# The second feed-forward's end in an order of its own, with a shorter inverse root, in an encoder layer on one core

## The chip, the core and the metric

The kernel runs on one core of a Trainium2 chip. TensorE (PE in the profile) multiplies matrices, VectorE (DVE), ScalarE (ACT) and GpSimd (POOL) work on elements, and SyncE (SP) issues nearly all DMAs. SBUF is the working memory of 128 partitions, PSUM holds the eight banks into which PE accumulates. The metric is the device time of one execution in microseconds (us): the median of three runs before the change, and beside it one profiled execution, whose trace all rows come from.

## The reference

One encoder layer is applied to two sequences of 512 tokens by 1024 channels, with the same weights: `y_prompt` from `x_prompt`, `y_sample` from `x_sample`.

```
x = x + 0.5 * swiglu(rms_norm(x, ffn1_norm), ...)            # first feed-forward
h = rms_norm(x, mix_norm); proj = h @ w_in; ...              # attention and mLSTM memory, merged
x = x + merged @ w_out
x = x + 0.5 * swiglu(rms_norm(x, ffn2_norm), ...)            # second feed-forward
return rms_norm(x, final_norm)

rms_norm(x, g) = x * rsqrt(mean(x * x, axis=-1) + 1e-6) * g
swiglu(x, wg, wu, wd) = (silu(x @ wg) * (x @ wu)) @ wd       # inner width 2816
```

Each query and key head, each memory head and the first three norms need an inverse root too.

## The kernel before, in words

**Stages.** The first feed-forward treats both sequences together; then come the mixing blocks of the two sequences (attention with eight heads, the mLSTM memory with four, gates, output projection), which overlap by hand; then the second feed-forward, and the final norm at its end. All matrix products are made of a high and a low part in `float32r`, three matmuls per product.

**The feed-forwards.** Gate/up and down products use a seven-product scheme (Strassen-Winograd) over the two sequences and the two halves of the inner dimension: B11, B21, B22, T4, T1, T2_, T3. `ffn_down` (line 449) runs the down product in the order of `DOWN`: B11, B21, T2_, T3, T4, T1, B22, for four chunks of the inner dimension, 28 steps in all. Each step fills four PSUM banks, d = 0 to 3, one for each block of 128 tokens, 128 partitions by 512 channels. `flush_` (line 542) evicts a bank as soon as it is finished, adding 0.5 times the bank to an accumulator in SBUF (line 550, a `scalar_tensor_tensor` of VectorE). T1 and B22 share the same banks, B22 accumulating on top of T1, so a bank goes on with B22 when its T1 sum has been read.

**The end of the last chunk.** In the last seven steps `flush_` calls `done(s, h, d)` when half h (512 channels) of block d of sequence s is complete: (0, 0) behind B21, (0, 1) behind T4, (1, 1) behind T1, and (1, 0) behind B22, the last step. For the second feed-forward this is `done2` (line 1346). It squares the half on ScalarE with a sum per row (`square`, line 1160), multiplies it by its half of `final_norm` in place (line 1349: on VectorE for (1, 0), else on GpSimd), and, when the blocks concerned are complete, makes the row scale (`row_scale`, line 1169, then `rstd_cols`) for four blocks of the first sequence or for two of the second, scales whole blocks of 1024 channels (line 1363 on ScalarE; line 1361 on VectorE for the last block of the second sequence) and stores each block with one DMA of SyncE (line 1364, 512 KB).

**The inverse root.** `rstd_cols` (line 151) takes sums of squares, one column for each block or head, divides by the width and adds 1e-6 (line 159), makes a first guess by integer operations on the bits (lines 161 and 163) and sharpens it three times (lines 167, 168, 170): 1 + 2 + 9 = 12 small operations of VectorE, each waiting for the one before. It is called 21 times: twice at the head (`norm_x`, where the inputs are normed before they are transposed), in the norms between the stages, for query and key heads, once for each memory head (`mem_out`, whose result PE then spreads over the partitions at line 187), and three times at the end. Its tiles come from pools of five buffers for each width.

**What sets the order.** A scheduler places the instructions on each engine's queue by a priority, which follows the order of the program text; `shifted` moves it, and `pin` (`tc.keep_in_program_order`) keeps pinned instructions in the order of the text among themselves. Each engine then works its queue strictly in order. The attention of the first sequence stands between 690 and 830 us: scores at line 914, their maxima at 917, transposes of the weights at 935 and products with the values at 942; the queries' transposes are at line 856, behind the rotation (lines 725 to 736) and the split (line 591), and matmuls of gates (line 686) are dealt in between.

Of the kernel before, what the change touches and what calls it, by code (L numbers as in the profile page):

```python
# [16 lines left out]
P = 128  # L17
S = 512
D = 1024
# [3 lines left out]
EPS = 1e-6  # L23
# [3 lines left out]
def encoder(ctx, tc, I, outs):  # L27
    nc = tc.nc
# [5 lines left out]
    spool = ctx.enter_context(tc.tile_pool(name="spool", bufs=4))  # L34
# [7 lines left out]
    def nm(s):  # L42
        n_id[0] += 1
        return f"{s}_{n_id[0]}"
# [100 lines left out]
    def emit_hl(src, g, k, xh, xl):  # L145
# [2 lines left out]
                                       op0=ALU.mult, op1=ALU.subtract)  # L148
        return i1, i2

    def rstd_cols(v, width, n):


        def t_(dt=F32):
            w = max(width, 4)
            return spool.tile([P, w], dt, tag=f"rs{w}", bufs=5, name=nm("rs"))[:, 0:width]
        V = nc.vector
        a = t_()
        V.tensor_scalar(a, v, 1.0 / n, EPS, op0=ALU.mult, op1=ALU.add)
        b = t_(I32)  # L160
        V.tensor_scalar(b, a.bitcast(I32), 1, None, op0=ALU.logical_shift_right)
        y_ = t_(I32)
        V.tensor_scalar(y_, b, -1.0, 1597463007.0, op0=ALU.mult, op1=ALU.add)
        y = y_.bitcast(F32)
        for _ in range(3):
            t = t_()
            V.scalar_tensor_tensor(t, y, -0.5, y, op0=ALU.mult, op1=ALU.mult)
            V.tensor_tensor(t, t, a, op=ALU.mult)
            r = t_()
            V.scalar_tensor_tensor(r, t, 1.5, y, op0=ALU.add, op1=ALU.mult)  # L170
            y = r
        return y

    def col_sums(acc, bs=(0, 1, 2, 3)):
        p = PT()
# [42 lines left out]
    V_ = nc.vector  # L218
    G_ = nc.gpsimd
    HK_ = KD // 2  # L220

    B11, B21, B22, T4, T1, T2_, T3 = range(7)
# [223 lines left out]
    DH = KD // 2  # L446
    n_steps = len(DOWN) * len(CHUNKS)

    def ffn_down(wd, rb, ring, tail, xres, done, at_step, hook):
# [88 lines left out]
        def add(t, u):  # L538
            V_.tensor_tensor(t, t, u, op=ALU.add)

        def flush_(i, d, p):
            m, last = DOWN[i % 7], i >= n - 7
            acc = {B11: e16[:, d], T2_: e16[:, DH + d], T1: e5[:, d], B21: xs[0][:, d], T4: xs[0][:, DH + d],
                   T3: xs[1][:, DH + d], B22: xs[1][:, d]}[m]
            if last and m == T1:
                acc = xs[1][:, DH + d]
            if i < 7 and m in (B11, T2_, T1):
                nc.scalar.activation(acc, p, AF.Copy, scale=0.5)
            else:
                V_.scalar_tensor_tensor(acc, p, 0.5, acc, op0=ALU.mult, op1=ALU.add)  # L550
# [583 lines left out]
    pin = tc.keep_in_program_order  # L1134
# [3 lines left out]
    x2buf = [dpool.tile([P, 2, 4, S], F32, name=f"x2buf{s}") for s in range(2)]  # L1138
    rbuf = [[dpool.tile([P, 7, 2, S], F32, name=f"rbuf{n}_{j}") for j in range(NF // 2)] for n in range(2)]
# [3 lines left out]
    up = Up(xc, I["ffn1_w_gate"], I["ffn1_w_up"], rbuf[0])  # L1143
# [14 lines left out]
    def square(x, to):  # L1158

        nc.scalar.activation(T2(F32, "f2"), x, AF.Square, accum_out=to)  # L1160

    def sums_tile():
        return spool.tile([P, 2, 4], F32, tag="sqs", bufs=6, name=nm("sqs"))

    def row_scale(sq, n=slice(0, 4)):

        w = n.stop - n.start
        t = spool.tile([P, 4], F32, tag="cs4", bufs=4, name=nm("rsum"))[:, 0:w]
        V_.tensor_tensor(t, sq[:, 0, n], sq[:, 1, n], op=ALU.add)
        return rstd_cols(t, w, D)  # L1170
# [97 lines left out]
    def done1(s, h, b):  # L1268
        x_ = xs[s][:, h * 4 + b, :]
        nc.sync.dma_start(xbuf[s][:, h, b, :], x_)  # L1270
# [51 lines left out]
    up = Up(xc, I["ffn2_w_gate"], I["ffn2_w_up"], rbuf[1])  # L1322
# [15 lines left out]
    tail = up.rest(raw0)  # L1338
    fn = []
# [3 lines left out]
        for half in range(2):  # L1343
            nc.gpsimd.dma_start(fn[half], I["final_norm"][half * S:(half + 1) * S].partition_broadcast(P))

    def done2(s, h, b):
        x_ = xs[s][:, h * 4 + b, :]
        square(x_, ssq3[s][:, h, b:b + 1])
        (V_ if (s, h) == (1, 0) else G_).tensor_tensor(x_, x_, fn[h], op=ALU.mult)
        if s == 0 and h == 1 and b == 3:  # L1350
            n = slice(0, 4)
        elif s == 1 and h == 0 and b % 2:
            n = slice(b - 1, b + 1)
        else:
            return
        r = row_scale(ssq3[s], n)
        for i in range(n.start, n.stop):
            v = xs[s].rearrange("p (h b) c -> p h b c", h=2)[:, :, i, :]
            r_ = r[:, i - n.start:i - n.start + 1]
            if s and i == 3:  # L1360
                V_.tensor_scalar(v, v, r_, None, op0=ALU.mult)
            else:
                nc.scalar.activation(v, v, AF.Copy, scale=r_)
            nc.sync.dma_start(outs[s][0, i * P:(i + 1) * P, :].rearrange("p (h c) -> p h c", h=2), v)

    ffn_down(I["ffn2_w_down"][0], rbuf[1], up.ring, tail, lambda s, h: x2buf[s][:, h], done2, n_steps - 14, load_fn)


def host_consts():
# [62 lines left out]
```

## Time and profile before

| what | us |
|---|---|
| median of three runs | 2118.5 (2116.89 to 2118.99) |
| profiled execution, its own time | 2116.6 |
| span of the profiled execution | 2114.8 |
| TensorE busy in it | 2068.3 (98%) |
| VectorE busy | 1558.7 (74%) |
| ScalarE busy | 940.2 (44%) |
| last matmul's end | 2100.4 |
| last operation's end (ScalarE's scaling) | 2109.0 |

The span runs from the first instruction to the last; the 1.8 us around it belong to the execution's own time. A row of the timeline gives start, duration, engine, line, operation, output and input, and in square brackets how long the engine was idle before and what ended that. A row of stretches gives, for a piece of the span, its length and then the busy time with the number of instructions of PE, of its weight loads, of VectorE, ScalarE and GpSimd, the clock granted to TensorE, the DMA engines' busy share and GB/s. A row of a group gives the count, the busy time, the mean duration in ns and the idle time before.

### The profile page before, as it was taken

How to read it: one execution, taken by the hardware profiler on the slowest of the kernel's cores; microseconds unless marked ns; L12 is line 12 of the kernel's file. 1: busy time of each engine (PE TensorE's matmuls, PEld its weight loads, DVE VectorE, ACT ScalarE, POOL GpSimd, SP SyncE). 2: the span in 40 equal slices, each digit the busy share in tenths (PEclk: the TensorE clock that was granted, in tenths of full speed). 3: DMA queues.
4: the chain of work that ended last, by engine and by line, in shares of the span. 5: the costliest groups of instructions: out<-in, count | busy, mean ns of one | idle time of the engine just before them, and what ended most of it. 6: DMA issues, size and time to landing. Idle time of an engine off the chain costs nothing.

```text
span 2114.8 us, 26230 instructions
## 1 busy us (share of the span) xinstructions
PE 2068.3 (98%) x9472; PEld 1692.4 (80%) x9472; DVE 1558.7 (74%) x2583; ACT 940.2 (44%) x1565; POOL 103.2 (5%) x110
## 2 busy tenths in 40 slices
PE   6999999999999999999999999999999999999997
PEld 5888888888888777878887787788888888888885
DVE  7888787776796896574649855754887877786696
ACT  6443443442225566463436555544544434343223
POOL 1000000001000110000101101010000000000002
PEclk9999999999999999999999999999999999999999
DMA  7464653489764222232341222354546545379763
GB/s 268 151 223 166 209 179 140 148 325 379 266 229 140 76 75 77 82 119 83 111 160 59 72 97 72 130 164 163 171 163 205 198 160 179 130 277 396 264 212 123
DMA packets 137425, 361.76 MB, mean 171 GB/s; under 512 B 13296, under 2 KB 13312, under 8 KB 136272
## 3 DMA queue, kind: packets, MB, share of 16 engines
q1 hardware_dynamic: 136704, 358.83, 48.6%
q0 software_dynamic: 592, 1.27, 0.2%
q8 instruction: 74, 1.21, 0.2%
q14 instruction: 55, 0.45, 0.1%
HBM read 255.15 MB, written 104.89 MB: 170 GB/s over the span
## 4 chain that ended last, share of the span: by engine, by line
PE 86%; DVE 7%; ACT 3%; DMA 2%; issue 1%; SPq 0%; POOL 0%; DVEq 0%; ACTq 0%; POOLq 0%
PE pss L283 17%; PE mm L686 14%; PE pst L283 11%; PE mm L283 10%; PE mm L533 7%; PE mm L670 4%; PE pst L533 4%; PE pss L533 4%; PE mm L1115 3%; PE pso L533 2%; PE pso L942 2%; PE pso L670 1%; PE pso L1071 1%; PE pss L914 1%; PE pss L1022 1%; PE pso L1115 1%
## 5 line engine op out<-in xcount | busy, mean ns | idle before, releaser
L283 PE MATMUL pss<-xc,w 128*128 128x512 f32 x1584 | 379.1, 389 | 0.0
L283 PEld LDWEIGHTS pss<-xc,w 128*128 128x128 f32 x1584 | 297.2, 188 | 62.0 <-DVE t L313 0.2
L686 PE MATMUL mm<-xh,w 128*128 128x512 f32 x896 | 294.1, 397 | 0.0
L283 PE MATMUL mm<-xc,w 128*128 128x512 f32 x1056 | 254.7, 391 | 2.9 <-ACT f L292 2.2
L242 ACT ACTIVATE w<-wr 128x1024 fp32r<-128x1024 f32 x132 | 139.7, 1060 | 235.3 <-PE pst L283 142.0
L283 PEld LDWEIGHTS mm<-xc,w 128*128 128x128 f32 x1056 | 196.7, 188 | 47.8 <-ACT f L292 6.3
L205 DVE TENSOR_TENSOR w<-wr,w 128x1024 fp32r<-128x1024 f32 (+1 forms) x112 | 136.6, 1221 | 114.1 <-ACT w L204 108.9
L243 DVE TENSOR_TENSOR w<-wr,w 128x1024 fp32r<-128x1024 f32 x132 | 161.1, 1222 | 80.2 <-ACT w L242 79.9
L686 PEld LDWEIGHTS mm<-xh,w 128*128 128x128 f32 x896 | 167.8, 189 | 32.4
L533 PE MATMUL mm<-w,rt 128*128 128x512 f32 x792 | 185.6, 389 | 0.9 <-DMA rt<-rbuf 0.9
L686 PE MATMUL mm<-xl,w 128*128 128x512 f32 x448 | 177.5, 396 | 0.0
L533 PEld LDWEIGHTS mm<-w,rt 128*128 128x128 f32 x792 | 148.4, 188 | 32.2 <-DMA rt<-rbuf 1.5
L204 ACT ACTIVATE w<-wr 128x1024 fp32r<-128x1024 f32 (+1 forms) x112 | 114.6, 1030 | 113.5 <-PE pso L1115 35.0
L283 PE MATMUL pst<-xc,w 128*128 128x512 f32 x528 | 127.1, 389 | 0.0
L283 PE MATMUL pst<-xc,f 128*128 128x512 f32 x528 | 127.0, 389 | 0.0
L283 PEld LDWEIGHTS pst<-xc,w 128*128 128x128 f32 x528 | 99.0, 188 | 20.8 <-ACT t L316 0.3
L283 PEld LDWEIGHTS pst<-xc,f 128*128 128x128 f32 x528 | 99.1, 188 | 20.6
L590 ACT ACTIVATE w<-t 128x512 fp32r<-128x512 f32 x82 | 51.6, 632 | 121.8 <-PE pst L533 63.6
L590 ACT ACTIVATE w<-wr 128x512 fp32r<-128x512 f32 x72 | 44.6, 631 | 129.8 <-PE pso L533 65.7
L686 PEld LDWEIGHTS mm<-xl,w 128*128 128x128 f32 x448 | 84.6, 189 | 16.2
L533 PE MATMUL pss<-w,rt 128*128 128x512 f32 x396 | 95.2, 390 | 1.3 <-ACT w L590 1.3
L533 PE MATMUL pst<-w,rt 128*128 128x512 f32 x396 | 94.3, 389 | 0.0
(323 smaller groups left out, 3497.8 us busy)
## 6 DMA issues: line engine op xcount, KB each, us to landing
rt<-rbuf SPq DMA_DIRECT2D x154, 512.0 KB, 6.2
rbuf<-t SPq DMA_DIRECT2D x72, 512.0 KB, 3.2
wr<-in_ffn_w_gate_dram SPq DMA_DIRECT2D x56, 512.0 KB, 4.2
wr<-in_w_in_cols_dram SPq DMA_DIRECT2D x56, 512.0 KB, 3.5
wr<-in_ffn_w_up_dram SPq DMA_DIRECT2D x44, 512.0 KB, 3.5
rbuf<-f SPq DMA_DIRECT2D x30, 512.0 KB, 3.2
rbuf<-tab SPq DMA_DIRECT2D x30, 512.0 KB, 3.6
wr<-in_ffn_w_down_dram SPq DMA_DIRECT2D x48, 256.0 KB, 7.6
```

What stands on the lines that cost most here:

```text
L204: pin(nc.scalar.activation(hi, raw, AF.Copy))
L205: pin(lo_eng.tensor_tensor(lo, raw, f(hi), op=ALU.subtract))
L242: pin(nc.scalar.activation(t[:, 0], src, AF.Copy))
L243: pin(V_.tensor_tensor(t[:, 1], src, f(t[:, 0]), op=ALU.subtract))
L283: nc.tensor.matmul(p, a[:, k, :], xt[:, b, k, :], start=(first and k == 0 and i == 0), stop=(k == HK_ - 1 and i == 2), skip_group_check=True)
L533: nc.tensor.matmul(p, r[:, b, d * P:(d + 1) * P], u[:, a, :], start=(first and q == 0 and k == 0), stop=(q == len(us) - 1 and k == 2), ski ...
L590: nc.scalar.activation(hi, src, AF.Copy)
L670: nc.tensor.matmul(p[b][:, :N], a[:, k, bs], w_[:, kl, :], start=(k == 0 and i == 0), stop=(k == KD - 1 and i == 2))
L686: nc.tensor.matmul(p, a[:, k, :], b, start=(k == 0 and i == 0), stop=(k == n - 1 and i == 2))
L914: nc.tensor.matmul(p, qT[:, h, b * P:(b + 1) * P], kv[:, hk * 2 + j, :], start=(j == 0), stop=(j == 1))
L942: nc.tensor.matmul(po, Vst[:, kv_, hk, :], w, start=(kv_ == 0 and i == 0), stop=(kv_ == 3 and i == 1))
L1115: nc.tensor.matmul(p[b], a[:, k, bs], w_[:, k - k0, :], start=(k == 0 and i == 0), stop=(k == KD - 1 and i == 2))
```

## The change

The inverse root is split into `rs_tile`, `rstd_of` (which takes a pinning function) and `rstd_cols`. Behind the first guess it now makes one Newton step (three operations) and one step of third order (five), 11 operations with the first.

`ffn_down` gets an `ends` function for the last step, B22, of the last chunk; the first feed-forward has none. `done2` keeps the first sequence's squares and GpSimd multiplications, but holds its row scale back; behind T1's block b it squares that half, multiplies it into a spare tile (`e5`) on VectorE, and scales and stores block b of the first sequence. `ends2` does B22's blocks: eviction, square and multiplication into another tile (`e16`); behind block 1 a root for blocks 0 and 1 from the two sums of squares (`last_scale`); behind block 2 the scaling and storing of block 0 in two halves. Block 3 is evicted in two halves of 256 columns, one squared by ScalarE and one by VectorE; then block 1's halves are scaled, the root of blocks 2 and 3 is made, and their four halves are scaled and stored: half 0 of block 3 by one operation of VectorE that also multiplies by `final_norm`, half 1 of block 2 by VectorE, the two others by ScalarE, which also issues their stores itself. Stores of the second sequence are 256 KB each. These operations are pinned.

```diff
+    def rstd_of(a, width, pin=lambda i: i):
...
+        b = t_(I32)
+        pin(V.tensor_scalar(b, a.bitcast(I32), 1, None, op0=ALU.logical_shift_right))
+        y_ = t_(I32)
+        pin(V.tensor_scalar(y_, b, -1.0, 1597463007.0, op0=ALU.mult, op1=ALU.add))
+        y = y_.bitcast(F32)
+        t = t_()
+        pin(V.scalar_tensor_tensor(t, y, -0.5, y, op0=ALU.mult, op1=ALU.mult))
+        pin(V.tensor_tensor(t, t, a, op=ALU.mult))
+        pin(V.scalar_tensor_tensor(t, t, 1.5, y, op0=ALU.add, op1=ALU.mult))
+        y, t, p, q = t, y, b.bitcast(F32), t_()
+        pin(V.tensor_tensor(t, y, y, op=ALU.mult))
+        pin(V.tensor_tensor(t, t, a, op=ALU.mult))
+        pin(V.tensor_scalar(p, t, 0.375, -1.25, op0=ALU.mult, op1=ALU.add))
+        pin(V.tensor_tensor(p, p, t, op=ALU.mult))
+        pin(V.scalar_tensor_tensor(q, p, 1.875, y, op0=ALU.add, op1=ALU.mult))
+        return q
...
     def rstd_cols(v, width, n):
...
-        for _ in range(3):
-            t = t_()
-            V.scalar_tensor_tensor(t, y, -0.5, y, op0=ALU.mult, op1=ALU.mult)
-            V.tensor_tensor(t, t, a, op=ALU.mult)
-            r = t_()
-            V.scalar_tensor_tensor(r, t, 1.5, y, op0=ALU.add, op1=ALU.mult)
-            y = r
-        return y
+        a = rs_tile(width)
+        nc.vector.tensor_scalar(a, v, 1.0 / n, EPS, op0=ALU.mult, op1=ALU.add)
+        return rstd_of(a, width)
...
+            if last and m == B22 and ends:
+                ends(d, p, acc, e16, e5)
+                return
...
             elif m == T1:
-                done(1, 1, d)
+                done(1, 1, d, e5)
...
-    def done2(s, h, b):
+    half_ms, other_r = [None], []
+
+    def store(s, i, h, v, q=None):
+        return (q or nc.sync).dma_start(outs[s][0, i * P:(i + 1) * P, h * S:(h + 1) * S], v)
+
+    def done2(s, h, b, spare=None):
         x_ = xs[s][:, h * 4 + b, :]
-        square(x_, ssq3[s][:, h, b:b + 1])
-        (V_ if (s, h) == (1, 0) else G_).tensor_tensor(x_, x_, fn[h], op=ALU.mult)
-        if s == 0 and h == 1 and b == 3:
-            n = slice(0, 4)
-        elif s == 1 and h == 0 and b % 2:
-            n = slice(b - 1, b + 1)
-        else:
+        if s == 0:
+            square(x_, ssq3[s][:, h, b:b + 1])
+            G_.tensor_tensor(x_, x_, fn[h], op=ALU.mult)
+            if h and b == 3:
+                other_r.append(row_scale(ssq3[0]))
             return
-        r = row_scale(ssq3[s], n)
-        for i in range(n.start, n.stop):
-            v = xs[s].rearrange("p (h b) c -> p h b c", h=2)[:, :, i, :]
-            r_ = r[:, i - n.start:i - n.start + 1]
-            if s and i == 3:
-                V_.tensor_scalar(v, v, r_, None, op0=ALU.mult)
-            else:
-                nc.scalar.activation(v, v, AF.Copy, scale=r_)
-            nc.sync.dma_start(outs[s][0, i * P:(i + 1) * P, :].rearrange("p (h c) -> p h c", h=2), v)
...
+        pin(nc.scalar.activation(T2(F32, "f2"), x_, AF.Square, accum_out=ssq3[1][:, 1, b:b + 1]))
+        V_.tensor_tensor(spare[:, b], x_, fn[1], op=ALU.mult)
+        v = xs[0].rearrange("p (h b) c -> p h b c", h=2)[:, :, b, :]
+        pin(nc.scalar.activation(v, v, AF.Copy, scale=other_r[0][:, b:b + 1]))
+        nc.sync.dma_start(outs[0][0, b * P:(b + 1) * P, :].rearrange("p (h c) -> p h c", h=2), v)
+
+    def last_scale(b0):
...
+        a = rs_tile(2)
+        sq, hm = ssq3[1][:, 0, b0:b0 + 2], half_ms[0][:, b0:b0 + 2]
+        pin(V_.scalar_tensor_tensor(a, sq, 1.0 / D, hm, op0=ALU.mult, op1=ALU.add))
+        return rstd_of(a, 2, pin)
...
+    def ends2(b, p, acc, pre0, pre1):
...
+        def on_act(i, h, r, q=None):
+            v = (pre0, pre1)[h][:, i]
+            pin(nc.scalar.activation(v, v, AF.Copy, scale=r))
+            pin(store(1, i, h, v, q))
+
+        if b < 3:
+            pin(V_.scalar_tensor_tensor(acc, p, 0.5, acc, op0=ALU.mult, op1=ALU.add))
+            pin(nc.scalar.activation(junk, acc, AF.Square, accum_out=ssq))
+            pin(V_.tensor_tensor(pre0[:, b], acc, fn[0], op=ALU.mult))
+            if b == 1:
+                t = half_ms[0] = spool.tile([P, 4], F32, tag="cs4", bufs=4, name=nm("hm"))
+                pin(V_.tensor_scalar(t, ssq3[1][:, 1], 1.0 / D, EPS, op0=ALU.mult, op1=ALU.add))
+                first_r.append(last_scale(0))
+            if b == 2:
+                for h in range(2):
+                    on_act(0, h, first_r[0][:, 0:1])
+            return
+        for c in (slice(0, H), slice(H, S)):
+            pin(V_.scalar_tensor_tensor(acc[:, c], p[:, c], 0.5, acc[:, c], op0=ALU.mult, op1=ALU.add))
+            if c.start == 0:
+                pin(nc.scalar.activation(junk[:, c], acc[:, c], AF.Square, accum_out=ssq))
...
+        pin(V_.scalar_tensor_tensor(junk[:, H:], acc[:, H:], 1.0, acc[:, H:], op0=ALU.mult, op1=ALU.mult, accum_out=more))
+        pin(V_.scalar_tensor_tensor(hm, more, 1.0 / D, hm, op0=ALU.mult, op1=ALU.add))
+        for h in range(2):
+            on_act(1, h, first_r[0][:, 1:2])
+        r = last_scale(2)
+        pin(V_.scalar_tensor_tensor(acc, acc, r[:, 1:2], fn[0], op0=ALU.mult, op1=ALU.mult))
+        on_act(3, 1, r[:, 1:2], nc.scalar)
+        pin(store(1, 3, 0, acc))
+        pin(V_.tensor_scalar(pre1[:, 2], pre1[:, 2], r[:, 0:1], None, op0=ALU.mult))
+        pin(store(1, 2, 1, pre1[:, 2]))
+        on_act(2, 0, r[:, 0:1], nc.scalar)
```

More of the change, by code (lines that the diff above doesn't have):

```diff
@@ L149, in emit_hl, with rs_tile @@
         return i1, i2
[L151 to L172 removed]
+    def rs_tile(width, dt=F32):
+        w = max(width, 4)
+        return spool.tile([P, w], dt, tag=f"rs{w}", bufs=5, name=nm("rs"))[:, 0:width]
+    def rstd_of(a, width, pin=lambda i: i):
+        V = nc.vector
+        t_ = lambda dt=F32: rs_tile(width, dt)
+        b = t_(I32)
[14 more added lines that the diff above has]
+        return q
+    def rstd_cols(v, width, n):
+        a = rs_tile(width)
+        nc.vector.tensor_scalar(a, v, 1.0 / n, EPS, op0=ALU.mult, op1=ALU.add)
+        return rstd_of(a, width)
     def col_sums(acc, bs=(0, 1, 2, 3)):
@@ L447, in encoder, with ffn_down @@
     n_steps = len(DOWN) * len(CHUNKS)
-    def ffn_down(wd, rb, ring, tail, xres, done, at_step, hook):
+    def ffn_down(wd, rb, ring, tail, xres, done, at_step, hook, ends=None):
         n = n_steps
@@ new lines, in done2 @@
+        v = xs[0].rearrange("p (h b) c -> p h b c", h=2)[:, :, b, :]
[6 more added lines that the diff above has]
+        return rstd_of(a, 2, pin)
+    first_r = []
@@ new lines, in ends2 @@
+    def ends2(b, p, acc, pre0, pre1):
+        H = S // 2
+        ssq = ssq3[1][:, 0, b:b + 1]
+        junk = T2(F32, "f2")
+        def on_act(i, h, r, q=None):
[18 more added lines that the diff above has]
+                pin(nc.scalar.activation(junk[:, c], acc[:, c], AF.Square, accum_out=ssq))
+        hm = half_ms[0][:, 3:4]
+        more = spool.tile([P, 4], F32, tag="cs4", bufs=4, name=nm("more"))[:, 0:1]
+        pin(V_.scalar_tensor_tensor(junk[:, H:], acc[:, H:], 1.0, acc[:, H:], op0=ALU.mult, op1=ALU.mult, accum_out=more))
[9 more added lines that the diff above has]
+        on_act(2, 0, r[:, 0:1], nc.scalar)
@@ L1369, in host_consts @@
+    ffn_down(I["ffn2_w_down"][0], rbuf[1], up.ring, tail, lambda s, h: x2buf[s][:, h], done2, n_steps - 14, load_fn,
+             ends2)
 def host_consts():
```

3 lines of the change are left out of this document (1 added, 2 removed).

## Prediction

> **What bounds the kernel now.** The page first: the busy row and the chain that ended last.
>
> ```profile
> span 2114.8 us, 26230 instructions
> PE 2068.3 (98%) x9472; PEld 1692.4 (80%) x9472; DVE 1558.7 (74%) x2583; ACT 940.2 (44%) x1565; POOL 103.2 (5%) x110
> PE 86%; DVE 7%; ACT 3%; DMA 2%; issue 1%; SPq 0%; POOL 0%; DVEq 0%; ACTq 0%; POOLq 0%
> ```
>
> TensorE bounds nearly everything. An edit counts only where PE idles: at the head, in some waits of the mixing block, and behind the last matmul. Second, the table of stretches, laid around the last matmul's end.
>
> ```profile
> 2092.00:2100.40 8.40, 8.36 (x37) 6.57 (x36) 3.60 (x5) 6.08 (x13) 4.26 (x3) 1.00 0.66 250
> 2100.40:2109.10 8.70, 0.00 (x0) 0.00 (x0) 7.34 (x32) 4.78 (x7) 0.00 (x0) 0.73 0.23 88
> 2109.10:2114.80 5.70, 0.00 (x0) 0.00 (x0) 0.00 (x0) 0.00 (x0) 0.00 (x0) 0.50 0.62 234
> ```
>
> The tail is 14.4 us: 8.7 in which VectorE is busy 7.34, then 5.7 of stores alone. Third, its instructions in order of time.
>
> ```profile
> 2085.76 1.17 DVE L159 TENSOR_SCALAR rs<-rsum 128x4 f32<-128x4 f32 x1
> 2087.24 0.69 DVE L550 SCALAR_TENSOR_TENSOR xs<-mm,xs 128x512 f32<-128x512 f32 x1
> 2088.82 1.32 POOL L1349 TENSOR_TENSOR xs<-xs,tab 128x512 f32<-128x512 f32 x1 [1.92 <-ACT f L1160]
> 2089.01 1.14 DVE L167 SCALAR_TENSOR_TENSOR rs<-rs 128x4 f32<-128x4 f32 x1
> 2090.38 0.16 DVE L170 SCALAR_TENSOR_TENSOR rs<-rs,rs 128x4 f32<-128x4 f32 x1
> 2090.64 4.27 ACT L1363 ACTIVATE xs<-xs,rs 128x1024 f32<-128x1024 f32 x4 [1.90 <-DVE rs L170]
> 2094.28 0.69 DVE L550 SCALAR_TENSOR_TENSOR xs<-mm,xs 128x512 f32<-128x512 f32 x1 [1.35 <-PE mm L533]
> 2095.43 0.62 ACT L1160 ACTIVATE f<-xs 128x512 f32<-128x512 f32 x1
> 2095.95 0.19 ACT L1160 ACTIVATION_READ_ACCUMULATOR f<-xs 128x1 f32 x1
> 2095.60 4.26 POOL L1349 TENSOR_TENSOR xs<-xs,tab 128x512 f32<-128x512 f32 x3 [5.46 <-ACT f L1160]
> 2097.39 1.30 DVE L1349 TENSOR_TENSOR xs<-xs,tab 128x512 f32<-128x512 f32 x1 [2.42 <-ACT f L1160]
> 2098.16 2.20 PE L533 MATMUL pso<-w,rt 128*128 128x512 f32 x9
> 2100.09 0.69 DVE L1349 TENSOR_TENSOR xs<-xs,tab 128x512 f32<-128x512 f32 x1 [0.79 <-ACT f L1160]
> 2103.11 0.68 DVE L550 SCALAR_TENSOR_TENSOR xs<-pso,xs 128x512 f32<-128x512 f32 x1
> 2105.19 0.15 DVE L1169 TENSOR_TENSOR rsum<-sqs 128x2 f32<-128x2 f32 x1
> 2107.62 0.16 DVE L170 SCALAR_TENSOR_TENSOR rs<-rs,rs 128x2 f32<-128x2 f32 x1
> 2107.88 1.15 ACT L1363 ACTIVATE xs<-xs,rs 128x1024 f32<-128x1024 f32 x1 [0.95 <-DVE rs L170]
> ```
>
> The last bank is done at 2100.36 but evicted only at 2103.11, since VectorE works off what stands ahead. The last root's twelve steps run from 2105.19 to 2107.62, 0.20 us each. ScalarE's last scaling ends at 2109.03, and SyncE can then issue the third store of the second sequence. Last, the stores: issue times with their durations in ns, landing of the 512 KB stores and of 256 KB stores elsewhere in us, and the DMA share (last but one column) in three microseconds at the end.
>
> ```profile
> L1364 SPq DMA_DIRECT2D out_dram<-xs x8: 533/534/650, 2091.8 to 2109.7; - x8
> DMA to landing us min/median/max: 3.1/3.7/4.2
> L1270 SPq DMA_DIRECT2D xbuf<-xs x16: 319/320/320, 618.3 to 665.8; - x16
> DMA to landing us min/median/max: 2.0/2.8/4.5
> 2110.00:2111.00 1.00, 0.00 (x0) 0.00 (x0) 0.00 (x0) 0.00 (x0) 0.00 (x0) 0.50 0.76 285
> 2111.00:2112.00 1.00, 0.00 (x0) 0.00 (x0) 0.00 (x0) 0.00 (x0) 0.00 (x0) 0.50 0.99 381
> 2112.00:2113.00 1.00, 0.00 (x0) 0.00 (x0) 0.00 (x0) 0.00 (x0) 0.00 (x0) 0.50 0.98 373
> ```
>
> The last two 512 KB stores take 0.76+0.99+0.98 = 2.73 us at full share, from 2110.24 to about 2113.0. So 1.2 us lie between an issue's start and its data (0.65 behind an issue of 0.53), and 1.8 us between the last data and the end of the span.
>
> **The change, part by part. The tail.** I walk the new order of each engine with the durations above and these, for forms that the tail lacked:
>
> ```profile
> L1049 ACT ACTIVATE t<-t,dn 128x512 f32<-128x512 f32 x8 | 5.7, 708 | 0.0
> L590 ACT ACTIVATE t<-t 128x256 fp32r<-128x256 f32 x16 | 5.8, 410 | 6.5 <-DVE t L736 6.2
> L734 DVE TENSOR_TENSOR t<-t,tab 128x256 f32<-128x256 f32 x16 | 6.0, 416 | 0.0
> L923 DVE TENSOR_SCALAR t<-t,asm x64: 468/477/1549, 730.8 to 1218.2; 128x512 f32<-128x512 f32 x64
> L125 POOL DMA_DIRECT2D g<-in_ffn_norm_dram x1 | 1.1, 1094 | 0.8 <-POOLq L1419 0.8
> ```
>
> (1) First sequence's root. It starts at 2085.76 as before, one step shorter, but two of the new multiplications by final_norm (0.69 each, taken from GpSimd) and two evictions stand between its steps on VectorE. GpSimd's operation of 2088.82 is gone, and with it the stretch at 2089.01, which ended with it. Steps of 0.20 and multiplications of 0.61 to 0.69 behind the eviction of 2087.24 give a result at 2091.0 instead of 2090.54: 0.45 later. Are the moved multiplications 0.69 (row of 2100.09) or 1.30 (2097.39)? The long one lies beside GpSimd operations, and the new order has none from 2086.9 on, so 0.69; at 1.30 the two in this root would take 1.2 us off the gain. The Trainium skill ("SBUF — State Buffer", Who interferes with whom) has it that a VectorE operation with two SBUF inputs and a GpSimd one that reads SBUF exclude each other, whichever starts second waiting for the whole of the first; by that rule, too, the new multiplications are free of it.
>
> (2) ScalarE then alternates four scalings (1.04 apart) with the squares of T1's block (0.62 apart): 2091.1 + 4 x 1.66 = 2097.7, where B22's square of block 1 starts, and its sum is there at 2098.45. VectorE, which has evicted block 1 at 2097.1, waits for it: in its queue stand the root of blocks 0 and 1, and behind it the evictions of blocks 2 and 3. This wait, from 2097.9 to 2098.5, is new, and it sets all that follows.
>
> (3) Eleven steps of 0.20 give the first root at 2100.6; block 2 is evicted and multiplied to 2102.0; block 3 in two halves (0.42, by the rows of 256 columns, between 0.15 and 0.69) to 2102.7; its second half squared on VectorE to 2103.2. ScalarE squares block 2 at 2101.3, scales two halves (0.71 each) and squares block 3's first half from 2103.2 to 2103.7. The last root starts there, at 2103.72, after 2105.19 before, and ends at 2105.9, after 2107.78. Its last step rewrites the buffer of the first root, so it also waits for the scalings of block 1; these end at 2104.9, 0.8 us of slack.
>
> (4) Blocks 0 and 1 are stored in halves, four issues of SyncE behind ScalarE's scalings, the last at 2105.0 and moved by 2106.7: clear of what follows. VectorE scales two halves to 2106.65 and 2107.05, ScalarE one to 2106.65, then it issues that half's store, behind which its last scaling and its last store are queued. An issue by ScalarE is in no trace: between 0.32 (SyncE's of 256 KB) and 1.09 (GpSimd's longest); I take 0.32, the same kind of plain store. The last four stores start at 2106.7, 2106.7, 2107.1 and 2107.8; data from 2107.7 (0.65 behind an issue of 0.32), and the same 1 MB in 2.73 us ends at 2110.5, after 2113.0. **Tail: -2.5 us.** At 1.09 the last store starts at 2108.5 and the end is 2111.0: -2.0. If the half evictions cost nothing or 0.69 each, -3.0 or -2.0. With (2) a microsecond off either way: -1.5 to -3.5.
>
> **The shorter root elsewhere.** One step of 0.20 less in each of 18 others.
>
> ```profile
> PE pss L1155 <- DVE raw L1203: 13.4, 2, 11.0
> PE pst L187 <- DVE rs L170: 0.9, 2, 0.5
> ```
>
> The two at the head end in scalings that PE waits for: **-0.4**. In the mixing block two waits of PE end with a root: **-0.4**. The rest lies under PE's work; with its cover gone a step would cost 0.2.
>
> **The moved order in the mixing block.** The built order shows that the scheduler, given the shorter roots, deals the first sequence's attention anew on PE, VectorE and ScalarE: the same work, and three loads in SyncE's queue one to three places sooner.
>
> ```profile
> 690.00:740.00 50.00, 47.85 (x245) 38.39 (x244) 40.98 (x88) 27.49 (x55) 6.62 (x5) 1.00 0.23 71
> 740.00:830.00 90.00, 88.20 (x422) 68.31 (x422) 72.35 (x144) 52.37 (x107) 8.55 (x7) 1.00 0.22 68
> PE pst L856 <- DVE t L591: 2.1, 3, 0.8
> ```
>
> PE idles 2.15 + 1.80 = 3.95 us here. The query transposes (L856) come 2 matmuls later, 6 earlier, 4 earlier and 4 earlier; at some 0.21 us a matmul (422 in 88.2 us), the net 12 give up to 2.5 us more waiting if VectorE is no sooner. But VectorE's queue now has a weight split behind the rotation and not ahead of it, so its halves come about a microsecond (the split is 1024 wide) sooner. Bounds -3.5 and +3; I take **0**.
>
> **Sum.** -2.5 - 0.4 - 0.4 + 0 = -3.3 us. The profiled execution took 2116.6 (span 2114.8), so 2113.3; the three runs have their median at 2118.5 (2116.89 to 2118.99), 1.9 above it. Forecast for the median: 2118.5 - 3.3 = **2115.2**.
>
> **The rivals.** (A) The attention's new order wins or loses what it can. For winning: PE's waits there are VectorE's, which has less to do. 2115.2 - 2.5 = 2112.7. Against: the later waits are ScalarE's and a queue's. Losing 3 gives 2118.2.
>
> (B) The tail isn't shorter: ScalarE's alternation in (2) is late by more, the root of blocks 0 and 1 holds back the evictions behind it, and every microsecond goes through to the end. At 2.5 us late: 2117.7. For it: VectorE waits there in order. Against: the four scalings had 4.27 us in the same place.
>
> (C) The other side: the halves' stores don't overlap. The last store lands at about 2109.7 + 3.7 = 2113.4 now. Four of 256 KB, one behind the other from 2106.7 at their median of 2.8, land at 2117.9: +4.5, and 2118.5 + 4.5 - 0.8 = 2122.2. It decides from 1.7 us a store on; the shortest landing of one is 2.0. Against: two stores of 512 KB drained back to back at full share. The Trainium skill ("DMA: Bandwidth & Descriptors", Measured) advises transfers of 1 MiB and more and gives 64 KB a third of the peak, for loads issued from GpSimd; by that rule halving costs, and the time is C's. No run here shows it yet for stores.
>
> **How the numbers follow.** About 0.2% (4.2 us) is what a measurement can tell from no change: 2114.3 to 2122.7 is the same. Forecast 0.57, mostly the same, by its lower end faster (0.10); A winning 0.20 (faster), A losing 0.07 (same); B 0.09 (same); C 0.07, the longer half of it slower. So faster 0.30, same 0.66, slower 0.04. The range takes in A both ways and B: 2111.3 to 2118.6.
>
> **What would show it.** From the last matmul's end to the span's end 11.9 us, not 14.4; first sequence's root at 2091.0, last one 5.5 us behind the last matmul (now 7.4); VectorE waiting for ScalarE's square ahead of the first small root; last data 1.8 us before the end; ScalarE's issue at 0.32; PE's idle time between 690 and 830 at 4 us. A tail above 13 us or an idle time in the attention beyond 7 us makes the forecast wrong.

## The result, and the profile after

| what | before | after |
|---|---|---|
| median of 20 runs each, us | 2117.57 (2115.07 to 2120.94) | 2114.05 (2112.26 to 2116.78) |
| ratio, 95% interval | | 0.9982 (0.9976 to 0.9988) |
| profiled execution, us | 2116.6 | 2115.0 |
| span of it | 2114.8 | 2113.2 |
| last matmul's end in it | 2100.36 | 2101.89 |
| tail: from there to the span's end | 14.4 | 11.3 |

By the ratio the kernel became 3.8 us faster (2.5 to 5.1), by the medians 3.5; the forecast was 3.3. That is just inside the 0.2% which the prediction called the bound to no change, and to that outcome it had given 0.66; the interval leaves no change out all the same. The forecast median, 2115.2, stood on three runs of the kernel before with a median of 2118.5; the twenty have 2117.57, so 0.9 of the 1.15 us by which 2114.05 lies under the forecast is that base. The two profiles differ by 1.6 us only: the one of before lies 1.0 below its median, the one of after 1.0 above. So the profiles are compared stretch by stretch, and above all from the last matmul's end on.

The page of the changed kernel: the span, the busy row, and the shares of the chain that ended last.

```profile
span 2113.2 us, 26221 instructions
PE 2070.4 (98%) x9472; PEld 1694.7 (80%) x9472; DVE 1556.0 (74%) x2569; ACT 940.6 (45%) x1568; POOL 97.4 (5%) x106
PE 85%; DVE 7%; ACT 3%; DMA 3%; issue 1%; SPq 0%; POOL 0%; ACTq 0%; DVEq 0%; POOLq 0%
```

Nothing there has moved: TensorE still bounds all but the ends. The table of stretches around the last matmul's end, the last row of it the time behind the start of the last store's issue, and the last microsecond with data in it (last but one column the DMA engines' busy share):

```profile
2093.50:2101.90 8.40, 8.39 (x38) 6.60 (x36) 6.15 (x19) 6.38 (x14) 0.00 (x0) 1.00 0.66 250
2101.90:2109.30 7.40, 0.00 (x0) 0.00 (x0) 5.64 (x21) 5.01 (x10) 0.00 (x0) 0.70 0.42 158
2109.30:2113.20 3.90, 0.00 (x0) 0.00 (x0) 0.00 (x0) 0.00 (x0) 0.00 (x0) 0.50 0.64 239
2111.00:2112.00 1.00, 0.00 (x0) 0.00 (x0) 0.00 (x0) 0.00 (x0) 0.00 (x0) 0.50 0.75 281
```

VectorE did 3.60 us of work beside the last 8.4 us of matmuls before, and does 6.15 now; behind them 7.34 have become 5.64. GpSimd is idle. With 0.75 of that microsecond at the full rate, the last data leave at 2111.75. The engines' instructions in order of time, by the steps of the prediction:

```profile
2092.29 0.15 DVE L173 SCALAR_TENSOR_TENSOR rs<-rs,rs 128x4 f32<-128x4 f32 x1
2094.49 0.69 DVE L1370 TENSOR_TENSOR e<-xs,tab 128x512 f32<-128x512 f32 x1
2099.17 0.61 ACT L1397 ACTIVATE f<-xs 128x512 f32<-128x512 f32 x1
2099.69 2.20 PE L540 MATMUL pso<-w,rt 128*128 128x512 f32 x9
2099.91 0.16 DVE L1379 SCALAR_TENSOR_TENSOR rs<-sqs,hm 128x2 f32<-128x2 f32 x1 [0.56 <-ACT f L1397]
2101.96 0.68 DVE L1396 SCALAR_TENSOR_TENSOR xs<-mm,xs 128x512 f32<-128x512 f32 x1
2103.29 0.75 DVE L1408 SCALAR_TENSOR_TENSOR xs<-pso,xs 128x256 f32<-128x256 f32 x2
2105.12 0.16 DVE L1379 SCALAR_TENSOR_TENSOR rs<-sqs,hm 128x2 f32<-128x2 f32 x1 [0.42 <-ACT f L1410]
2106.90 0.16 DVE L172 TENSOR_TENSOR rs<-rs,rs 128x2 f32<-128x2 f32 x1
2107.17 0.16 DVE L173 SCALAR_TENSOR_TENSOR rs<-rs,rs 128x2 f32<-128x2 f32 x1
2108.12 0.40 ACTq L1359 DMA_DIRECT2D out_dram<-e  x1
2109.31 0.34 ACTq L1359 DMA_DIRECT2D out_dram<-e  x1
```

The new wait of VectorE ahead of the first small root is there (0.56, the first row of L1379), block 2's bank is evicted behind that root (2101.96), and block 3's, the last, at 2103.29. The last root is done at 2107.33, which is 5.4 us behind the last matmul; before it was 7.4.

### The profile page after: what moved, and what is told of

The parts are those of the page before. It is cut to its first block, busy times and chain, and to the rows that moved or that the text cites. A ratio compares the mean times of both kernels' runs of the same rounds, so it can differ in the third digit from the quotient of the medians.

```text
span 2113.2 us, 26221 instructions
## 1 busy us (share of the span) xinstructions
PE 2070.4 (98%) x9472; PEld 1694.7 (80%) x9472; DVE 1556.0 (74%) x2569; ACT 940.6 (45%) x1568; POOL 97.4 (5%) x106
## 4 chain that ended last, share of the span: by engine, by line
PE 85%; DVE 7%; ACT 3%; DMA 3%; issue 1%; SPq 0%; POOL 0%; ACTq 0%; DVEq 0%; POOLq 0%
PE pss L290 17%; PE mm L696 14%; PE pst L290 11%; PE mm L290 10%; PE mm L540 7%; PE mm L680 4%; PE pst L540 4%; PE pss L540 4%; PE mm L1125 3%; PE pso L540 2%; PE pso L952 2%; PE pso L680 1%; PE pss L924 1%; PE pso L1081 1%; PE pss L1032 1%
## 5 line engine op out<-in xcount | busy, mean ns | idle before, releaser
L540 PE MATMUL pss<-w,rt 128*128 128x512 f32 x396 | 95.3, 390 | 0.9 <-ACT w L600 0.9
```

The costliest lines, as they stand in the source:

```text
L540: nc.tensor.matmul(p, r[:, b, d * P:(d + 1) * P], u[:, a, :], start=(first and q == 0 and k == 0), stop=(q == len(us) - 1 and k == 2), ski ...
```

## The experiments

Each is read by its tail, the time from the last matmul's end to the span's end, since executions differ by more than that ahead of it: in the twelve profiles the last matmul ends between 2099.5 and 2104.4, in the two of the kernel before at 2100.4 and 2099.5. The tail repeats within 0.1 us where the end is the same: 14.4 twice for the kernel before, 11.4 and 11.3 in e1 and the changed kernel, 9.8 in e8 and e9. Times stand where a run was timed against the kernel before, with the ratio and its 95% interval; e3 to e7 and b2 have one execution each. PE's idle time is that between 690 and 830 us; the last column is the time between the starts of matmuls 3134 and 3574, counted in PE's order, between which the attention's order was dealt anew.

| kernel | tail | ratio | PE idle | matmuls 3134 to 3574 |
|---|---|---|---|---|
| before | 14.4 | | 3.95 | 94.5 |
| b2, before again | 14.4 | | 4.3 | 96.2 |
| e1, new end alone | 11.4 | 0.9987 (0.9978 to 0.9996) | 4.6 | 95.3 |
| e8, e9's end, before's attention | 9.8 | 0.9976 (0.9966 to 0.9986) | 5.65 | 96.4 |
| the changed kernel | 11.3 | 0.9982 (0.9976 to 0.9988) | 4.3 | 95.6 |
| e2, short root alone | 14.0 | 0.9994 (0.9986 to 1.0003) | 4.5 | 96.1 |
| e3, all stores by SyncE | 11.3 | | 5.3 | 96.7 |
| e4, multiplications on GpSimd | 10.9 | | 5.3 | 96.8 |
| e5, two scalings later | 10.9 | | 5.4 | 96.9 |
| e6, last block whole | 11.6 | | 5.3 | 96.6 |
| e7, stores whole | 12.0 | | 5.3 | 96.9 |
| e9, e5 with block 2 folded | 9.8 | 0.9973 (0.9964 to 0.9983) | 6.3 | 97.7 |

The first four rows have before's order in the attention, the others the new one.

**e1: the new end, the old root elsewhere.**

```diff
+    def rstd_cols(v, width, n, short=False):
...
+        if short:
+            return rstd_of(a, width)
...
+        for _ in range(3):
...
-                other_r.append(row_scale(ssq3[0]))
+                other_r.append(row_scale(ssq3[0], short=True))
```

> Before's 12-step root everywhere ahead of the last group of products, so that TensorE's order in the attention is that of before; the new end whole, with the short root in the three roots of the end. Theory (the gain is the end alone, and neither the attention's order nor the short roots elsewhere are worth anything): 3.1 us of the 3.5 us between the medians, a ratio of 0.9985 (0.9980 to 0.9990), and 11.1 to 11.6 us from the last matmul to the end of the span, as in the changed kernel (11.3). Rival (the attention's new order wins and the end gives little): 0.9990 to 1.000 and a tail of 13 us or more.

The end of PE in its timeline, under the line with its span:

```profile
core 0 of [0], span 2111.8 us
2098.23 2.20 PE L555 MATMUL pso<-w,rt 128*128 128x512 f32 x9
```

2111.8 - 2100.43 is a tail of 11.4, and by time 2.75 us are won (0.8 to 4.7). The end alone carries most of the gain, as the theory has it; the rival needed a tail of 13.

**e2: the short root everywhere, before's end.** Only `rstd_cols` is replaced by the change's three functions.

> The short root everywhere, before's end otherwise; TensorE's order in the attention is that of the changed kernel. Theory: the roots give 0.4 in the head or less, nothing in the attention, and in the end 0.45 us for the first sequence's root and 0.4 for the last: a ratio of 0.9993 to 1.0000, and 13.6 to 14.2 us from the last matmul to the end (14.4 before). Rival (the attention's order wins 2 us or more): 0.9985 or less. Rival (it loses, as the 1.1 us on the changed kernel's profile between the attention's first and last matmul suggest): 1.0000 to 1.0006, with that loss again between the same matmuls.

The same two rows:

```profile
core 0 of [0], span 2113.6 us
2097.41 2.20 PE L540 MATMUL pso<-w,rt 128*128 128x512 f32 x9
```

The tail is 14.0, shorter by 0.4; of the whole time 0.0006 is won, and the interval takes in no change. The gains of e1 and e2 by time, 0.0013 and 0.0006, come near the change's 0.0018 when added, though they overlap: both runs have the short root at the end. Neither rival on the attention's order is borne out by the time, but the interval is as wide as their claims. The sign of the second is there: matmuls 3134 to 3574 take 96.1 us, after 94.5 in before's first profile, but b2, with the old order, has 96.2.

**e7: the second sequence's blocks stored whole.** Each half's scaling writes into the block's place in `xs`, and one DMA of 512 KB follows the second half.

```diff
+        def whole(i, q):
+            pin(q.dma_start(outs[1][0, i * P:(i + 1) * P, :].rearrange("p (h c) -> p h c", h=2), both[:, :, i]))
...
-            pin(nc.scalar.activation(v, v, AF.Copy, scale=r))
-            pin(store(1, i, h, v, q))
+            pin(nc.scalar.activation(both[:, h, i], (pre0, pre1)[h][:, i], AF.Copy, scale=r))
+            if q:
+                whole(i, q)
```

> The changed kernel with the second sequence's four blocks stored whole, 512 KB each, when the second of their halves is scaled; the last one is issued by ScalarE as before this edit, so it starts at the same 7.4 us behind the last matmul, but moves both halves of block 2. Theory (halves let most of the data leave while the second half is being scaled, and 256 KB stores do overlap): the tail grows by 0.6 to 1.8 us, to 11.9 to 13.1 us. Rival (what a store costs is its start, so that four stores cost more than two and whole ones are better): 11.3 us or less.

Its last matmul, its last issue, and (in the second fence) the end of its DMA work:

```profile
core 0 of [0], span 2114.1 us
2099.86 2.20 PE L540 MATMUL pso<-w,rt 128*128 128x512 f32 x9
2108.91 0.64 ACTq L1398 DMA_DIRECT2D out_dram<-xs  x1
```

```profile
2111.00:2112.00 1.00, 0.00 (x0) 0.00 (x0) 0.00 (x0) 0.00 (x0) 0.00 (x0) 0.50 1.00 387
2112.00:2113.00 1.00, 0.00 (x0) 0.00 (x0) 0.00 (x0) 0.00 (x0) 0.00 (x0) 0.50 0.33 119
```

The tail is 12.0, although the last issue starts at 6.85 us behind the last matmul and not at 7.42 (no issue stands between ScalarE's last two scalings here): from its start to the end 5.2 us pass, and 3.9 in the changed kernel. So halves are worth 0.7 us, and rival C of the prediction, which had them land one behind the other, is refuted: in the changed kernel everything has landed 3.9 us behind the start of the last of four issues. The Trainium skill ("DMA: Bandwidth & Descriptors", Measured) advises 1 MiB and more; at this end, where the time behind the last issue counts and not the rate, the measurement goes the other way.

**e3: all stores by SyncE.**

```diff
-        on_act(3, 1, r[:, 1:2], nc.scalar)
+        on_act(3, 1, r[:, 1:2])
...
-        on_act(2, 0, r[:, 0:1], nc.scalar)
+        on_act(2, 0, r[:, 0:1])
```

> The changed kernel with all stores issued by SyncE, none by ScalarE. Theory (an issue takes SyncE 0.33 to 0.38 us and there is room between the four last ones, at 2108.1, 2108.6 and 2109.3): the tail stays within 0.4 us of 11.3 us, and ScalarE's last scaling begins up to 0.4 us earlier because no issue stands between its last two scalings, so 10.9 to 11.4 us. Rival (issues in one queue follow each other too closely and the last stores wait for the ones ahead): 11.8 us or more.

The span is 2112.1 and the last matmul ends at 2100.81: 11.3, no change. ScalarE's last two scalings follow each other without an issue between them (1.33 us from 2106.29), as expected, but SyncE's last two issues take 0.90 together from 2107.94 on, so the last of them starts at about 2108.45, which is 7.6 us behind the last matmul (7.4 in the changed kernel). What ScalarE gains by not issuing is lost in SyncE's queue; two stores by ScalarE are worth nothing that this shows.

**e4: the four new multiplications back on GpSimd.**

```diff
-        V_.tensor_tensor(spare[:, b], x_, fn[1], op=ALU.mult)
+        G_.tensor_tensor(spare[:, b], x_, fn[1], op=ALU.mult)
```

> The changed kernel with the four multiplications of the second sequence's upper half put back on GpSimd (0.69 us each on VectorE in the changed kernel). Theory of the prediction (VectorE works unhindered there only because GpSimd has nothing to do): VectorE's steps beside them stretch as in before, so that a 512-column operation of 0.7 us takes 1.2 to 1.4 us while GpSimd works, and the first sequence's root ends 0.3 us or more later behind its sums than the 5.2 us of the changed kernel. Rival (the two don't hinder each other; VectorE's long steps of before had another cause): the same durations as in the changed kernel, the root 2 to 3 us earlier behind its sums since 2.8 us of work have left VectorE. For the tail both expect 11.3 us within 0.6.

The timeline, from the first sequence's sums to the first small root:

```profile
2089.56 0.16 DVE L1179 TENSOR_TENSOR rsum<-sqs 128x4 f32<-128x4 f32 x1 [0.79 <-ACT f L1170]
2092.00 1.29 POOL L1370 TENSOR_TENSOR e<-xs,tab 128x512 f32<-128x512 f32 x1 [1.11 <-DVE rs L165]
2092.03 1.29 DVE L166 TENSOR_TENSOR rs<-rs,rs 128x4 f32<-128x4 f32 x1
2094.34 0.16 DVE L173 SCALAR_TENSOR_TENSOR rs<-rs,rs 128x4 f32<-128x4 f32 x1
2095.19 3.82 POOL L1370 TENSOR_TENSOR e<-xs,tab 128x512 f32<-128x512 f32 x3 [1.89 <-DVE xs L560]
2096.24 0.69 DVE L560 SCALAR_TENSOR_TENSOR xs<-pso,xs 128x512 f32<-128x512 f32 x1 [0.53 <-PE pso L540]
2101.97 0.16 DVE L1379 SCALAR_TENSOR_TENSOR rs<-sqs,hm 128x2 f32<-128x2 f32 x1 [0.15 <-ACT f L1397]
```

A step of the root, 0.15 us long in the changed kernel, starts 0.03 behind a GpSimd operation and takes 1.29, until that is done. An eviction, which reads PSUM and SBUF, keeps its 0.69 beside 3.82 us of GpSimd. The hindrance is real, then, but neither size was right: the root comes 4.8 us behind the sums (2089.56 to 2094.34), 0.4 earlier than the 5.2 of the changed kernel (2087.09 to 2092.29), since one stretch of 1.13 costs less than the two multiplications that have left VectorE's queue. VectorE's wait for ScalarE falls to 0.15, and the tail to 10.9. So this part of the change wins nothing: with the multiplications left on GpSimd the tail is 0.4 shorter. The rule that the prediction cited from the Trainium skill ("SBUF — State Buffer", Who interferes with whom) agrees with both rows: the step with two SBUF inputs waits for the GpSimd operation's end, the eviction with one SBUF input and one from PSUM does not. A single SBUF input alone does not keep an operation free, though: the root's first step, which reads and writes SBUF, took 1.17 us beside a GpSimd operation in before already (2085.76).

**e5: the scalings of the first sequence's blocks 2 and 3 moved behind the second sequence's square of block 1.**

```diff
+        if b < 2:
+            first_out(b)
...
             if b == 1:
+                first_out(2)
+                first_out(3)
```

> The changed kernel with the first sequence's scalings of blocks 2 and 3 (1.1 us each on ScalarE) and their stores moved behind the second sequence's square of block 1. Theory (ScalarE's alternation of squares and scalings is late by 0.6 us, VectorE waits for it ahead of the first small root, and the evictions of blocks 2 and 3 queue behind it): that wait of 0.56 us goes, the last eviction begins up to 0.5 us earlier and the tail is 10.6 to 11.1 us. Rival (the scalings moved stand in front of the second sequence's own scalings and make the last ones late): 11.3 to 12.5 us.

ScalarE's square of block 1 with the scalings behind it, VectorE around the first small root, the last matmul:

```profile
core 0 of [0], span 2113.2 us
2099.02 0.63 ACT L1401 ACTIVATE f<-xs 128x512 f32<-128x512 f32 x1 [1.26 <-DVE xs L1400]
2099.65 2.17 ACT L1376 ACTIVATE xs<-xs,rs 128x1024 f32<-128x1024 f32 x2
2099.90 0.16 DVE L1383 SCALAR_TENSOR_TENSOR rs<-sqs,hm 128x2 f32<-128x2 f32 x1
2100.14 2.20 PE L540 MATMUL pso<-w,rt 128*128 128x512 f32 x9
2105.11 0.16 DVE L1383 SCALAR_TENSOR_TENSOR rs<-sqs,hm 128x2 f32<-128x2 f32 x1 [0.42 <-ACT f L1416]
```

The wait of 0.56 is gone: ScalarE now waits for VectorE (1.26). The small root starts 2.44 us ahead of the last matmul's end, not 1.98, and the tail is shorter by the same 0.4 to 0.5. Step (2) of the prediction did set all that followed.

**e6: the last block evicted and squared whole.**

```diff
-        for c in (slice(0, H), slice(H, S)):
-            pin(V_.scalar_tensor_tensor(acc[:, c], p[:, c], 0.5, acc[:, c], op0=ALU.mult, op1=ALU.add))
...
+        pin(V_.scalar_tensor_tensor(acc, p, 0.5, acc, op0=ALU.mult, op1=ALU.add))
+        pin(nc.scalar.activation(junk, acc, AF.Square, accum_out=ssq))
```

> The changed kernel with the last block evicted in one instruction of 512 columns and squared whole by ScalarE. Theory (halves let ScalarE square one half while VectorE evicts and squares the other): now 0.72 us of eviction and then 0.62 of square in a row, with a crossing between engines of some 0.1, against 0.75 + 0.42 us by halves and 0.42 of waiting, which the whole square saves as VectorE does nothing of it: by these rows the root starts 1.5 to 1.6 us behind the eviction's start, against 1.83 in the changed kernel (2103.29 to 2105.12), so the tail is 10.9 to 11.3 us. Rival (the halves are worth what they were made for): the root starts 2.1 us or more behind the eviction's start, and the tail is 11.6 us or more.

The timeline from the last eviction to the last root's start:

```profile
2102.90 0.68 DVE L1406 SCALAR_TENSOR_TENSOR xs<-pso,xs 128x512 f32<-128x512 f32 x1
2102.98 1.32 ACT L1391 ACTIVATE e<-e,rs 128x512 f32<-128x512 f32 x2
2104.21 0.61 ACT L1407 ACTIVATE f<-xs 128x512 f32<-128x512 f32 x1
2104.95 0.16 DVE L1379 SCALAR_TENSOR_TENSOR rs<-sqs,hm 128x2 f32<-128x2 f32 x1 [1.36 <-ACT f L1407]
```

My theory fell: 2.05 us from the eviction's start to the root's, against 1.83, and a tail of 11.6, the rival's, whose 2.1 us is missed by little. I had added up the operations and forgotten what stands ahead of the square in ScalarE's queue: block 0's two scalings, until 2104.21. The same queue makes the 0.42 us of waiting in the changed kernel: the square of the first half, evicted by about 2103.7, starts at 2104.59, behind the scalings of block 0. e9 moves it ahead of them.

**e9: e5, and out of the way what stands ahead of the last root.** Block 2's lower half isn't multiplied by `final_norm` ahead of block 3's eviction; VectorE multiplies it by norm and root at once at the end, and ScalarE scales that block's upper half. ScalarE squares block 3's first half ahead of three of the four scalings of blocks 0 and 1. **e8** is the same with before's root in the attention's two calls.

```diff
+            if b == 2:
+                mid.append(acc)
+                on_act(0, 0, first_r[0][:, 0:1])
...
+            if b < 2:
+                pin(V_.tensor_tensor(pre0[:, b], acc, fn[0], op=ALU.mult))
...
+        pin(V_.scalar_tensor_tensor(mid[0], mid[0], r[:, 0:1], fn[0], op0=ALU.mult, op1=ALU.mult))
+        pin(store(1, 2, 0, mid[0]))
+        on_act(2, 1, r[:, 0:1], nc.scalar)
```

> e5, and of block 2's lower half no multiplication ahead of the last eviction (VectorE multiplies it by norm and root at once at the end, 0.75 us, as it does for block 3), ScalarE's square of block 3's first half ahead of three of the four scalings of blocks 0 and 1. Theory (the end is a chain on VectorE from the second small root to the last: 0.69 us of multiplication ahead of the last eviction and 0.42 us of waiting for ScalarE stand in it): the last eviction 0.6 us earlier behind the first small root, the wait under 0.2, so the last root 0.8 to 1.0 us earlier and a tail of 9.8 to 10.3 us, against 10.9 in e5 and 11.3 in the changed kernel; by times a ratio of 0.9975 to 0.9985 here and, if the attention's order costs 1 to 2 us, 0.0005 to 0.0009 less in e8. Rival (the scalings that are moved back make ScalarE late behind the last root): 10.5 us or more.

> The end of e9 below, and the short root everywhere but in the attention's two roots of 8 and 32 columns, which keep before's 12 steps; TensorE's order between the attention's products 3134 and 3574 is then before's, instruction by instruction. So far those products take 1.12 to 2.44 us longer than in before's profile in the seven profiles that have the new order (mean 2.05), and 0 and 0.82 in the two that have the old one. Theory (the new order costs 1 to 2 us there): 0 to 0.9 us in this run. Rival (before's one profile was a lucky one and the order costs nothing): 1.2 to 2.4 us. For the end see e9.

> The kernel before once more, for a second profile of its old order in the attention. Theory (the order costs 1 to 2 us): the products 3134 to 3574 take within 0.9 us of what they took in before's first profile. Rival (that one was lucky): 1.2 us or more above it. Tail 14.4 us within 0.1 for both.

The end of e9 in its timeline:

```profile
core 0 of [0], span 2112.2 us
2100.20 2.20 PE L540 MATMUL pso<-w,rt 128*128 128x512 f32 x9
2102.62 0.75 DVE L1415 SCALAR_TENSOR_TENSOR xs<-pso,xs 128x256 f32<-128x256 f32 x2
2103.43 0.40 ACT L1417 ACTIVATE f<-xs 128x256 f32<-128x256 f32 x1
2104.13 0.16 DVE L1383 SCALAR_TENSOR_TENSOR rs<-sqs,hm 128x2 f32<-128x2 f32 x1
```

The last eviction begins 0.22 us behind the last matmul (2102.62), where the changed kernel took 1.40; the wait ahead of the last root is gone; the tail is 9.8, 4.6 less than before and 1.5 less than the changed kernel, 0.5 of it from e5's edit and the rest from e9's two further ones together. By time the ratio is 0.9973, some 5.7 us. That is faster than the kernel before; over the changed kernel only the tail shows a gain, since the intervals of the two ratios overlap. e8 has the same tail and 0.9976, so giving the attention its old order wins nothing that these times show.

On the order itself the theory fell, too. The old order took 95.3, 96.2 and 96.4 us between matmuls 3134 and 3574 in e1, b2 and e8; the last two fall on the rival's side (1.7 and 2.0 above before's first profile), so that profile lies at the low end of what the old order takes. The new order's eight profiles have a mean of 96.7, the old order's four one of 95.6, each with a spread of about 2. So the profiles give the new order 1.1 us more, hardly beyond what the spreads allow. Profiles taken together on one chip agree in the sign: the new order is longer by 0.9 and 1.6 us in e2 and e7 against e1, and by 1.6 and 1.3 in e9 against b2 and e8. The times of e8 and e9 don't show it. A cost of about a microsecond is likely, then, but open; that the new order wins is borne out by neither.

## Why the prediction was right, point by point

**The tail, forecast -2.5, measured -3.1.** (1) On before's clock (the last matmul is 1.53 later in the profile of after) the first sequence's root ends at 2090.9, forecast 2091.0; the multiplications take 0.69, as chosen, with GpSimd idle. No run shows whether 1.30 would have taken 1.2 us off: e4 takes the other way round the hindrance and gains 0.4, a way that the prediction didn't weigh. (2) VectorE's wait for the square of block 1 was forecast at 0.6 and is 0.56, and by e5 it goes through to the end. (3) The last root ends 5.4 us behind the last matmul, forecast 5.5. (4) Here is the mis-sized term. ScalarE's issues take 0.40 and 0.34 (0.32 was taken). The last data leave at 2110.2 on before's clock, forecast 2110.5; and from the last data to the end 1.5 us pass, where I had carried over 1.8 from before. These two, 0.3 us each, make the 0.6. The 0.1 of (3) is used up ahead of the last issue, which starts 7.42 us behind the last matmul, forecast 7.44.

**The short root elsewhere, forecast -0.4 and -0.4: the first can't be shown, the second failed.** At the head the step is gone as priced: 12.52 to 14.71 us for the first root, after 12.52 to 14.91. PE's two waits there have a mean of 13.3 us in the three profiles with the old root and of 12.9 in the nine with the short one. With the start of the hundredth matmul in before's first profile taken as 0, it lies at 0, 0.18 and 0.78 with the old root and between -0.15 and +0.35, around a mean of 0, with the short one. The means differ by the forecast's size, but the spreads are as wide, and the clock differs there too: between 35 and 40 us it was 1.00 in before's first profile and 0.66 to 0.79 in the other eleven.

In the mixing block "two waits of PE end with a root" did not become shorter. PE's waits by what ended them, of the changed kernel:

```profile
PE pss L1165 <- DVE raw L1213: 13.0, 2, 10.8
PE pst L194 <- DVE rs L173: 1.2, 3, 0.5
```

The second row was 0.9 in two waits. All idle time ahead of the eight groups of matmuls that spread a memory head's root (line 187 before, 194 after), whatever ended it, is 6.3 us before and 6.4 after. The step that failed is to let PE's wait shrink by what the root gets shorter. The roots are shorter: the first runs from 872.36 to 874.70 before and from 872.54 to 874.70 after. But PE's queue was laid anew: in seven of the eight places the spreading matmuls stand one matmul sooner in PE's order. The first place, what PE does ahead of them and they themselves, before and after:

```profile
874.33 0.39 PE L686 MATMUL mm<-xl,w 128*128 128x512 f32 x1
874.85 0.62 PE L187 MATMUL pst<-ident,rs 128*128 128x128 f32 x4
```

```profile
874.06 0.61 PE L696 MATMUL mm<-xh,w 128*128 128x512 f32 x2
874.85 0.62 PE L194 MATMUL pst<-ident,rs 128*128 128x128 f32 x4 [0.18 <-DVE rs L173]
```

PE has one matmul less to do ahead of them, does it behind them, and waits as long as before: the step of 0.2 us is filled by the order, not won.

**The attention's order, forecast 0.** The stretches of the changed kernel:

```profile
690.00:740.00 50.00, 47.15 (x242) 37.66 (x242) 39.16 (x81) 25.37 (x49) 7.71 (x5) 1.00 0.22 69
740.00:830.00 90.00, 88.55 (x421) 67.94 (x420) 72.12 (x149) 54.39 (x112) 7.61 (x6) 1.00 0.21 68
```

PE idles 2.85 + 1.45 = 4.3 us, forecast 4; the other seven profiles of this order have 4.5 to 6.3. PE's waits between 700 and 830 us in the changed kernel:

```profile
PE pss L924 <- ACT t L931: 2.1, 3, 1.4
PE pst L866 <- DVE t L601: 0.5, 1, 0.5
```

The wait of the query transposes, which stand net 12 matmuls sooner, fell from 2.1 us to 0.5 (to 1.6 in six of the other seven profiles). VectorE was sooner, then, and by more than the microsecond that was forecast: its halves for the last three groups of them start at 716.4, 720.7 and 725.7 us, after 718.5, 722.3 and 727.2. In its place the scores wait for ScalarE's exponentials: 2.0 to 2.3 us in all eight profiles of the new order, at most 0.8 in the four of the old one. That is what rival A had against itself. The guess at zero between -3.5 and +3 held within about a microsecond, but as two changes against each other, which the prediction had not sized.

**The sum.** -3.1 in the tail, something between 0 and -0.4 in the head, and 0 to +1 in the attention make -2.1 to -3.5; the medians have -3.5, and their interval reaches to 2.5. The forecast was near by luck in part: a tail gain too small by 0.6 stood beside 0.4 to 0.8 of roots that are not seen.

**The rivals.** A: neither 2.5 won nor 3 lost; about 1 may be lost. B: the alternation was late by just what the forecast held. C: refuted by e7.

## What to carry to other kernels

Behind the last matmul, walk each engine's queue in order and ask of every instruction whether the last root needs it; what it doesn't need goes behind it or into the time before, and a square that another engine waits for goes ahead of scalings that nobody waits for (e9: 1.5 us more by such moves together). Work that is moved to an engine on the last chain should pay for its place there (e4: left on GpSimd, four multiplications cost 0.4 us less). Halve the last stores so that data leave while the other half is being scaled. A step shortened in the middle of the program is worth nothing until PE's idle time there is seen to shrink, since the scheduler may lay the order anew around it.

## What the runs showed of the hardware

From the last data, reckoned by the DMA share as running at the full rate to their end, to the end of the span some 1.5 us pass where the last store has 256 KB (the changed kernel, e1, e3 to e6, e8, e9: 1.45 to 1.55) and 1.8 where it has 512 KB (before, b2, e2, e7: 1.75 to 1.8).

A step of the root that waits for a second engine as well starts 0.26 to 0.27 us behind the one ahead of it and not 0.20, though the other engine was done long before (2106.90 to 2107.17 in the changed kernel, the scalings having ended at 2106.3); without that second wait e9 has 0.19.

The clock granted to TensorE, as the stretches give it, need not be the pace of its matmuls where it starts. Between 15 and 25 us the granted clock is 0.81 in before's first profile, 0.79 in e7 and 1.00 in the ten others; but in all twelve the transposes at the head, which start at 15.3 to 15.9 us, follow each other by 0.21 us and come to 0.11 to 0.16 only between 18.7 and 20.8 us.
